# A mixture of a dense and a gathered expert layer: groups of two columns, three more gather tiles, earlier transposes, larger packets

## The chip, the cores and the metric

The kernel runs on one core of a Trainium2 chip. A core has TensorE (PE), VectorE (DVE), ScalarE (ACT), GpSimd (POOL) and SyncE (SP), which each work through their own instructions in a fixed order, and 16 DMA engines. The metric is the device time of one execution in microseconds (us); the median of several runs is compared.

## What is computed

A block of a network for 1024 tokens of 1024 channels: a mixer (sliding means and a gated part), and then a layer of 16,384 experts of which each token uses 128 (8 heads with 16 choices each). The second part, cut to what matters:

```python
def peer_ffn(h, wq, keys, u_tab, v_tab):        # block of 128 tokens
    q = (xb @ wq).reshape(T, PEER_HEADS, 2, D_HALF)
    s = jnp.einsum('thpd,phkd->thpk', q, keys)
    s_top, i_top = lax.top_k(s, PEER_TOPK)
    ...
    idx = jnp.take_along_axis(cand_i, best_pos, axis=-1)
    gate = jax.nn.softmax(best_s, axis=-1)
    u = u_tab[idx]
    v = v_tab[idx]
    act = jax.nn.gelu(jnp.einsum('td,thkd->thk', xb, u))
    return jnp.einsum('thk,thkd->td', gate * act, v)
```

All values are float32. The two tables u_tab and v_tab (peer_u, peer_v) hold 16,384 rows of 4 KB each.

## The kernel before

The tokens are eight blocks of 128. Blocks 2 to 5 (512 tokens) are done densely: every expert is computed for them, as 128 columns of 128 experts, and a gate that is zero for the experts not chosen is multiplied in. Blocks 0, 1, 6 and 7 are done sparsely: the chosen rows are gathered from the tables.

Ahead of both stands the mixer and the scoring. `project` (line 159) multiplies by the weights w_in, w_out and wq; each call loads two tiles w of 512 KB (line 164) in four buffers, with runs of 256 floats, 1 KB. It notes its last matmul in the list `marks`. Scoring gives per block the chosen experts (`pick`, line 383), and `turn` (line 465) transposes them.

The gate of the dense part is made by `gates_dense` (line 557): for four tokens at a time VectorE writes one-hot rows (oh), ScalarE scales them, TensorE multiplies them into a 128x128 map per token; 32 tokens make a tile gs of 2 MB that goes to G in DRAM (line 580). G is laid out by group of four columns first, so that a write goes out in runs of 512 B, and the load gc of four columns (line 647) reads 1 MB that lies together, in runs of 512 B.

`dense` (line 612) walks over the 128 columns. For each it loads raw_u and raw_v (512 KB each, three buffers together, lines 636 and 641), splits each into a high and a low part (ACT writes uh or vh, VectorE writes ul or vl, line 131), makes 24 matmuls into mu (`mm3`, lines 138 to 140: three products for each of 8 slices), then the gelu (ACT, line 652), the product with the gate (VectorE, line 653) and the split of that into wh and wl. When GROUP = 3 columns are ready, `down` (line 623) makes for each of 8 output parts 9 matmuls into one tile mm of the on-chip sums, and VectorE adds that into hD (line 631). vh, vl, wh and wl have GROUP buffers each.

A sparse block b has two halves. `sparse_u` (called Ub, line 494): 128 gathers of one row per token (a tile of 128 x 1024, 0.5 MB, issued by GpSimd, line 483), each followed by a product with a sum on VectorE (junk, line 504); then w is made and transposed into wT (lines 511 and 513). `sparse_v` (Vb, line 516): 32 quads; GpSimd copies a column of wT into one of four small tiles wz (line 523), gathers four tiles, and TensorE makes eight matmuls with them into po (line 534). The last closes the block (`finish`, line 548).

The gathered rows lie in ROWS = 7 tiles rowt and, once the first stage's memory is free, also in VROWS = 4 tiles rowv. Where U and V halves run together, U uses rowv and V uses rowt (line 680); else both are used in turn. EARLY and LATE (lines 56 and 57) say in which order the halves are written: U0, then V0 with half of U1 in the first stage; then, spread over the columns of `dense`, the rest of U1, V1 with U6, V6 with U7, and V7. The program is written in that order, and a scheduler (Tile, with its own model of times) puts the instructions of each engine into the final order; `anchors` (line 814) hold a transposition of w or a quad behind a chosen entry of `marks`.

Of the kernel before, what the change touches and what calls it, by code (L numbers as in the profile page):

```python
# [8 lines left out]
F32 = mybir.dt.float32  # L9
# [8 lines left out]
P = 128  # L18
# [3 lines left out]
HALF = 512  # L22
# [5 lines left out]
NK = 128  # L28
# [4 lines left out]
WC = 256  # L33
# [6 lines left out]
ND = N * len(MIDDLE)  # L40
DBLK = ND // P
d0 = D0 // P
GROUP = 3
TB = 4
GT = 32
GI = 4
# [5 lines left out]

ROWS, VROWS = 7, 4
QUAD = 4

EARLY = ({"U0": 128}, {"V0": 128, "U1": 64})
LATE = ({"U1": 64}, {"V1": 128, "U6": 128}, {"V6": 128, "U7": 128}, {"V7": 128})
# [6 lines left out]
def hybrid_block(ctx: ExitStack, tc: tile.TileContext, t: dict, out: bass.AP):  # L64
# [21 lines left out]
    wz = []  # L86
    for i in range(4):
        z = const.tile([P, 4, 63], F32, name=f"wz{i}")
        nc.gpsimd.memset(z, 0.0)
        wz.append(z)  # L90
# [17 lines left out]

    G = dram.tile([NK // GI, ND // GT, P, GI, GT], F32, name="G")

# [48 lines left out]
    def project(fr, name, col, xs, by_token):  # L159

        ws = []
        for half in range(2):
            w = fr.tile([P, 4, WC], F32, name="w", bufs=4)
            nc.sync.dma_start(w, t[name][half * HALF:(half + 1) * HALF, col:col + WC]
                              .rearrange("(c p) e -> p c e", p=P))
            ws.append(w)
        res = []
        for x in xs:
            dst = ps.tile([P, 2, N], F32, name="mm")
            for i in range(2):  # L170
                part = slice(i * P, (i + 1) * P)
                for c in range(NDC):
                    w = ws[c // 4][:, c % 4, :]
                    lhs, rhs = (x[:, c, part], w) if by_token else (w[:, part], x[:, c, :])
                    mm = nc.tensor.matmul(dst[:, i, :], lhs, rhs, start=c == 0, stop=c == NDC - 1)  # L175
            res.append(dst)
        marks.append(mm.ins)
        flush()
        return res
# [336 lines left out]
    def sparse_v(b):  # L516
# [4 lines left out]
        for j in range(32):  # L521
            z = wz[j % len(wz)]
            nc.gpsimd.tensor_copy(z[:, :, 31:32], wg[:, :, j:j + 1])

            rows_ = []
            for g in range(QUAD):
                rows_.append(gather("peer_v", idxT[:, g * 32 + j:g * 32 + j + 1], j))
                if g < QUAD - 1:
                    yield
            with behind(f"V{b}", j) or tc.high_priority():  # L530
                first = None
                for g, (r, _) in enumerate(rows_):
                    for q in range(2):
                        mm = nc.tensor.matmul(po[g * 32:(g + 1) * 32, q * HALF:(q + 1) * HALF],  # L534
                                              z[:, g, 31 - j:63 - j], r[:, q * HALF:(q + 1) * HALF],
                                              start=j == 0, stop=j == 31)
                        first = first or mm
# [19 lines left out]
    def gates_dense(gp, b):  # L557

        iT = turned[b]
        for part in range(P // GT):  # L560
            kb = (b - d0) * (P // GT) + part
            gs = gp.tile([P, NK, GT], F32, name="gs", bufs=2)
            for t0 in range(0, GT, TB):
# [9 lines left out]
                for i in range(TB):  # L573
# [5 lines left out]
                yield  # L579
            nc.sync.dma_start(G[:, kb].rearrange("a i b t -> i a (b t)"),  # L580
                              gs.rearrange("i (a b) t -> i a (b t)", b=GI))

# [29 lines left out]
    def dense(de, xdh, xdl):  # L612
# [3 lines left out]
        with tc.tile_pool(name="da", bufs=2, side="right", reuse_waits="tile") as da:  # L616
# [17 lines left out]
            for c in range(NK):  # L634
# [10 lines left out]
                if c % GI == 0:  # L645
                    gc = da.tile([P, ND // GT, GI, GT], F32, name="gc")
                    nc.sync.dma_start(gc.rearrange("i k b t -> i k (b t)"),
                                      G[c // GI].rearrange("k i b t -> i k (b t)"))
                p = ps1.tile([P, ND], F32, name="mu", bufs=2)
# [163 lines left out]
    rts.close()  # L813
    anchors.update({"U0": [marks[BEHIND[0]]], "V0": marks[BEHIND[0]::BEHIND[1]]})
    for _ in sparse(EARLY):
# [52 lines left out]
```

## Time and profile before

| what | us |
|---|---|
| median of three runs | 2639.56 |
| the three runs | 2629.94 to 2653.57 |
| the profiled execution | 2627.74 |
| its span, first to last instruction | 2625.9 |
| PE busy / DVE busy / POOL busy / ACT busy | 2415.2 / 1851.3 / 1264.0 / 766.9 |

The profile is of one execution. Busy time is the time in which an engine has at least one instruction at work; DMA share is the mean busy share of the 16 DMA engines, which can come out a little above 1 where packets overlap. Granted clock 1.00 is TensorE at 2.4 GHz, the lower level is 1.2 GHz. A wait is idle time of an engine, put down to what ended it.

### The profile page before, as it was taken

How to read it: one execution, taken by the hardware profiler on the slowest of the kernel's cores; microseconds unless marked ns; L12 is line 12 of the kernel's file. 1: busy time of each engine (PE TensorE's matmuls, PEld its weight loads, DVE VectorE, ACT ScalarE, POOL GpSimd, SP SyncE). 2: the span in 40 equal slices, each digit the busy share in tenths (PEclk: the TensorE clock that was granted, in tenths of full speed). 3: DMA queues.
4: the chain of work that ended last, by engine and by line, in shares of the span. 5: the costliest groups of instructions: out<-in, count | busy, mean ns of one | idle time of the engine just before them, and what ended most of it. 6: DMA issues, size and time to landing. Idle time of an engine off the chain costs nothing.

```text
span 2625.9 us, 34296 instructions
## 1 busy us (share of the span) xinstructions
PE 2415.2 (92%) x11968; PEld 1861.7 (71%) x11968; DVE 1851.3 (71%) x4251; ACT 766.9 (29%) x1420; POOL 1264.0 (48%) x1228
## 2 busy tenths in 40 slices
PE   7997999889985669999999999999999999999993
PEld 6886788767763547788777777777777777776660
DVE  2389979987978956799766766666677667664332
ACT  2221011247754632222222222222222222222110
POOL 0034744034455544455655565555555555644553
PEclk9998999999987789999999999999999999999997
DMA  7677999579998898999999999999989999988986
GB/s 242 219 245 231 376 340 305 181 247 364 328 327 287 286 344 291 333 343 352 344 354 356 350 332 349 350 351 337 365 327 348 361 333 349 349 333 321 324 317 240
DMA packets 348397, 835.65 MB, mean 318 GB/s; under 512 B 25153, under 2 KB 160833, under 8 KB 348225
## 3 DMA queue, kind: packets, MB, share of 16 engines
q0 software_dynamic: 147456, 536.94, 55.4%
q1 hardware_dynamic: 200768, 296.53, 33.0%
q8 instruction: 95, 1.56, 0.2%
q14 instruction: 78, 0.63, 0.1%
HBM read 787.23 MB, written 46.14 MB: 317 GB/s over the span
## 4 chain that ended last, share of the span: by engine, by line
PE 67%; DVE 15%; DMA 10%; issue 4%; ACT 1%; POOL 1%; SPq 0%; POOLq 0%; DVEq 0%; ACTq 0%
PE mm L138 8%; PE mu L140 8%; PE mm L139 8%; PE mu L138 8%; PE mm L140 8%; PE mu L139 8%; PE po L534 8%; PE mm L175 8%; DVE junk L504 3%; DVE oh L567 2%; DMA raw_u<-uT 2%; DMA rowt<-peer_u,idx 2%; DVE rest L375 1%; DMA rowv<-peer_u,idx 1%; DMA rowv<-peer_v,idxT 1%
## 5 line engine op out<-in xcount | busy, mean ns | idle before, releaser
L483 POOL DMA_INDIRECT rowt<-peer_v,idxT x448 | 511.0, 1141 | 649.1 <-PE po L534 393.6
L483 POOL DMA_INDIRECT rowt<-peer_u,idx x224 | 274.6, 1226 | 357.0 <-DVE top L373 165.4
L483 POOL DMA_INDIRECT rowv<-peer_u,idx x288 | 355.6, 1235 | 156.4 <-DVE junk L504 96.0
L138 PE MATMUL mm<-vh,wh 128*128 128x512 f32 x1024 | 398.1, 395 | 17.2 <-ACT wh L130 17.0
L138 PE MATMUL mu<-xdh,uh 128*128 128x512 f32 x1024 | 401.3, 392 | 4.0 <-ACT uh L130 4.0
L140 PE MATMUL mu<-xdh,ul 128*128 128x512 f32 x1024 | 401.7, 392 | 0.5 <-DVE ul L131 0.5
L139 PE MATMUL mm<-vl,wh 128*128 128x512 f32 x1024 | 400.5, 392 | 0.0
L139 PE MATMUL mu<-xdl,uh 128*128 128x512 f32 x1024 | 400.2, 391 | 0.0
L504 DVE SCALAR_TENSOR_TENSOR junk<-rowv,h 128x1024 bf16<-128x1024 f32 x288 | 351.5, 1221 | 60.2 <-DMA rowv<-peer_u,idx 57.8
L631 DVE TENSOR_TENSOR hD<-hD,mm 128x512 f32<-128x512 f32 x344 | 226.3, 683 | 213.6 <-PE mm L140 213.2
L140 PE MATMUL mm<-vh,wl 128*128 128x512 f32 x1024 | 374.1, 391 | 0.1
L504 DVE SCALAR_TENSOR_TENSOR junk<-rowt,h 128x1024 bf16<-128x1024 f32 x224 | 272.3, 1215 | 28.1 <-DMA rowt<-peer_u,idx 26.8
L652 ACT ACTIVATE a<-mu 128x512 f32<-128x512 f32 x128 | 76.3, 596 | 600.4 <-PE mu L140 600.0
L138 PEld LDWEIGHTS mm<-vh,wh 128*128 128x128 f32 x1024 | 193.3, 189 | 79.9 <-ACT wh L130 19.4
L534 PE MATMUL po<-rowt,wz 128*32 128x512 f32 x1792 | 232.4, 611 | 17.1 <-DMA rowt<-peer_v,idxT 13.6
L140 PEld LDWEIGHTS mu<-xdh,ul 128*128 128x128 f32 x1024 | 192.2, 188 | 59.2 <-issue 8.4
L138 PEld LDWEIGHTS mu<-xdh,uh 128*128 128x128 f32 x1024 | 192.2, 188 | 55.1 <-issue 10.9
L140 PEld LDWEIGHTS mm<-vh,wl 128*128 128x128 f32 x1024 | 191.9, 188 | 49.6 <-issue 8.4
L139 PEld LDWEIGHTS mu<-xdl,uh 128*128 128x128 f32 x1024 | 192.2, 188 | 48.0 <-issue 8.4
L139 PEld LDWEIGHTS mm<-vl,wh 128*128 128x128 f32 x1024 | 193.4, 189 | 44.5 <-issue 4.2
L131 DVE SCALAR_TENSOR_TENSOR ul<-raw_u,uh 128x1024 fp32r<-128x1024 f32 x128 | 156.4, 1222 | 44.4 <-ACT uh L130 42.7
L130 ACT ACTIVATE vh<-raw_v 128x1024 fp32r<-128x1024 f32 x128 | 130.0, 1048 | 176.4 <-PE mm L140 149.9
(162 smaller groups left out, 3323.0 us busy)
## 6 DMA issues: line engine op xcount, KB each, us to landing
raw_u<-uT SPq DMA_DIRECT2D x128, 512.0 KB, 7.0
raw_v<-peer_v SPq DMA_DIRECT2D x128, 512.0 KB, 6.9
G<-gs SPq DMA_DIRECT2D x16, 2048.0 KB, 16.8
w<-wq SPq DMA_DIRECT2D x48, 512.0 KB, 6.9
w<-w_in SPq DMA_DIRECT2D x36, 512.0 KB, 4.7
w<-w_out SPq DMA_DIRECT2D x24, 512.0 KB, 7.2
h<-x SPq DMA_DIRECT2D x16, 512.0 KB, 11.6
rowt<-peer_v,idxT POOLq DMA_INDIRECT x448
```

Of the source, the lines that this page charges most:

```text
L130: nc.scalar.activation(hi, src, AF.Copy)
L131: nc.vector.scalar_tensor_tensor(lo, src, 1.0, f32(hi), op0=ALU.mult, op1=ALU.subtract)
L138: nc.tensor.matmul(dst, lh, rh, start=first and c == 0, stop=False)
L139: nc.tensor.matmul(dst, lh, rl, start=False, stop=False)
L140: nc.tensor.matmul(dst, ll, rh, start=False, stop=last and c == n - 1)
L175: mm = nc.tensor.matmul(dst[:, i, :], lhs, rhs, start=c == 0, stop=c == NDC - 1)
L483: ins = nc.gpsimd.indirect_dma_start(out=rowt, out_offset=None, in_=t[table], in_offset=bass.IndirectOffsetOnAxis(ap=ids, axis=0))
L504: nc.vector.scalar_tensor_tensor(junk, r, 1.0, h, op0=ALU.mult, op1=ALU.mult, accum_out=act[:, j:j + 1])
L534: mm = nc.tensor.matmul(po[g * 32:(g + 1) * 32, q * HALF:(q + 1) * HALF], z[:, g, 31 - j:63 - j], r[:, q * HALF:(q + 1) * HALF], start=j = ...
L567: nc.vector.tensor_tensor(oh, iota_k[:, None, None, :].to_broadcast([P, 2, TB, NK]), iT[:, 0:2, tok:tok + TB, None].to_broadcast([P, 2, TB ...
L631: nc.vector.tensor_add(hq, hq, p)
L652: nc.scalar.activation(a, p, AF.Gelu_apprx_tanh)
```

## The change

Five things are changed. GROUP is 2 instead of 3: `down` runs every second column, with 6 matmuls for each of its 8 output parts, and there are two buffers of vh, vl, wh and wl. ROWS is 8 instead of 7, VROWS is 7 instead of 4, and there are three tiles wz instead of four. In EARLY 16 gathers of U1 stand between U0 and V0, and the transposition of block 0's w is held behind `marks[1]` instead of `marks[4]`. In `sparse_v` the copy into wz comes behind the four gathers of its quad. And the weights w are packed on the host so that each partition's part of a tile is one run of 4 KB, and G is laid out by 32 tokens, partition, column and token, so that gs is written in one run of 16 KB a partition, while gc still reads runs of 512 B.

```diff
-GROUP = 3
+GROUP = 2
...
-ROWS, VROWS = 7, 4
+ROWS, VROWS = 8, 7
 QUAD = 4
 
-EARLY = ({"U0": 128}, {"V0": 128, "U1": 64})
+EARLY = ({"U0": 128}, {"U1": 16}, {"V0": 128, "U1": 48})
...
-    for i in range(4):
+    for i in range(3):
         z = const.tile([P, 4, 63], F32, name=f"wz{i}")
...
-    G = dram.tile([NK // GI, ND // GT, P, GI, GT], F32, name="G")
+    G = dram.tile([ND // GT, P, NK, GT], F32, name="G")
...
-            nc.sync.dma_start(w, t[name][half * HALF:(half + 1) * HALF, col:col + WC]
-                              .rearrange("(c p) e -> p c e", p=P))
+            nc.sync.dma_start(w.rearrange("p c e -> p (c e)"), t[name][col // WC, half])
...
         for j in range(32):
-            z = wz[j % len(wz)]
-            nc.gpsimd.tensor_copy(z[:, :, 31:32], wg[:, :, j:j + 1])
 
             rows_ = []
             for g in range(QUAD):
                 rows_.append(gather("peer_v", idxT[:, g * 32 + j:g * 32 + j + 1], j))
                 if g < QUAD - 1:
                     yield
+            z = wz[j % len(wz)]
+            nc.gpsimd.tensor_copy(z[:, :, 31:32], wg[:, :, j:j + 1])
...
-            nc.sync.dma_start(G[:, kb].rearrange("a i b t -> i a (b t)"),
-                              gs.rearrange("i (a b) t -> i a (b t)", b=GI))
+            nc.sync.dma_start(G[kb].rearrange("i k t -> i (k t)"), gs.rearrange("i k t -> i (k t)"))
...
-                                      G[c // GI].rearrange("k i b t -> i k (b t)"))
+                                      G[:, :, c:c + GI, :].rearrange("k i b t -> i k (b t)"))
...
-    anchors.update({"U0": [marks[BEHIND[0]]], "V0": marks[BEHIND[0]::BEHIND[1]]})
+    anchors.update({"U0": [marks[1]], "V0": marks[BEHIND[0]::BEHIND[1]]})
...
+    def packed(w):
+
+        w = np.asarray(w)[0]
+        return c(w.reshape(2, 4, P, w.shape[1] // WC, WC).transpose(3, 0, 2, 1, 4).reshape(-1, 2, P, 4 * WC))
...
-        "w_in": c(np.asarray(w_in)[0]),
+        "w_in": packed(w_in),
```

w_out and wq are packed in the same way.

The scheduler makes a new order for every engine. At the end of TensorE's order of before stand these rows (mm is a part of `down`, a po row is one quad with a tile of rowv or rowt).

```order
L138 MATMUL mm<-vh,wh 128x512
L139 MATMUL mm<-vl,wh 128x512
L140 MATMUL mm<-vh,wl 128x512
L534 MATMUL po<-rowv,wz_87 32x512 x8
L534 MATMUL po<-rowt,wz_89 32x512 x8
L534 MATMUL po<-rowv,wz_91 32x512 x8
L534 MATMUL po<-rowt,wz_93 32x512 x8
L534 MATMUL po<-rowv,wz_87 32x512 x8
L534 MATMUL po<-rowt,wz_89 32x512 x8
L534 MATMUL po<-rowv,wz_91 32x512 x8
L534 MATMUL po<-rowt,wz_93 32x512 x8
```

And these stand there now, at the end of TensorE's order of the changed kernel.

```order
L139 MATMUL mm<-vl,wh 128x512
L140 MATMUL mm<-vh,wl 128x512
L138 MATMUL mm<-vh,wh 128x512
L139 MATMUL mm<-vl,wh 128x512
L140 MATMUL mm<-vh,wl 128x512
L138 MATMUL mm<-vh,wh 128x512
L139 MATMUL mm<-vl,wh 128x512
L140 MATMUL mm<-vh,wl 128x512
```

The eight quads that stood behind the last column are gone from there: the last quad now stands where 100.7 columns have had their matmuls into mu.

On VectorE, in the stretch of columns that V1 and U6 share, the order of before has this (hD_7475 to hD_7478 are the four blocks of the dense output, in two halves each; junk is a product with a gathered tile).

```order
L631 TENSOR_TENSOR hD_7475<-hD_7475,mm 128x512 x2
L631 TENSOR_TENSOR hD_7476<-hD_7476,mm 128x512 x2
L131 SCALAR_TENSOR_TENSOR ul<-raw_u,uh 128x1024
L653 TENSOR_TENSOR a<-a,gc 128x512
L631 TENSOR_TENSOR hD_7477<-hD_7477,mm 128x512 x2
L631 TENSOR_TENSOR hD_7478<-hD_7478,mm 128x512
L131 SCALAR_TENSOR_TENSOR wl<-a,wh 128x512
L131 SCALAR_TENSOR_TENSOR vl<-raw_v,vh 128x1024
L504 SCALAR_TENSOR_TENSOR junk,act<-rowv,h 128x1024
L131 SCALAR_TENSOR_TENSOR vl<-raw_v,vh 128x1024
L631 TENSOR_TENSOR hD_7478<-hD_7478,mm 128x512
L504 SCALAR_TENSOR_TENSOR junk,act<-rowv,h 128x1024 x3
```

VectorE's order of the changed kernel in the same stretch, where the four blocks are hD_7473 to hD_7476:

```order
L629 TENSOR_TENSOR hD_7473<-hD_7473,mm 128x512 x2
L503 SCALAR_TENSOR_TENSOR junk,act<-rowv,h 128x1024
L629 TENSOR_TENSOR hD_7474<-hD_7474,mm 128x512 x2
L503 SCALAR_TENSOR_TENSOR junk,act<-rowv,h 128x1024 x3
L629 TENSOR_TENSOR hD_7475<-hD_7475,mm 128x512
L503 SCALAR_TENSOR_TENSOR junk,act<-rowv,h 128x1024
L629 TENSOR_TENSOR hD_7475<-hD_7475,mm 128x512
L629 TENSOR_TENSOR hD_7476<-hD_7476,mm 128x512 x2
L131 SCALAR_TENSOR_TENSOR vl<-raw_v,vh 128x1024
L651 TENSOR_TENSOR a<-a,gc 128x512
L131 SCALAR_TENSOR_TENSOR wl<-a,wh 128x512
L131 SCALAR_TENSOR_TENSOR ul<-raw_u,uh 128x1024
```

The eight additions of a group now come every second column, and more products stand beside fewer columns: U6's 128 products are spread over some 25 columns, where they were spread over some 45.

On GpSimd, where U0 ends and V0 begins, the order of before has this (peer_u gathers are U0's and then U1's, peer_v gathers are V0's, the copies are the waits for wT).

```order
L483 DMA rowt<-peer_u,idx 128x1024 x129
L483 DMA rowt<-peer_v,idxT 128x1024 x4
L483 DMA rowt<-peer_u,idx 128x1024 x2
L483 DMA rowt<-peer_v,idxT 128x1024 x3
L523 COPY wz_87<-wT 128x4
L523 COPY wz_89<-wT 128x4
L523 COPY wz_91<-wT 128x4
L523 COPY wz_93<-wT 128x4
```

GpSimd's order of the changed kernel at the same place:

```order
L482 DMA rowt<-peer_u,idx 128x1024 x145
L482 DMA rowt<-peer_v,idxT 128x1024 x4
L482 DMA rowt<-peer_u,idx 128x1024
L482 DMA rowt<-peer_v,idxT 128x1024 x2
L528 COPY wz_87<-wT 128x4
L528 COPY wz_89<-wT 128x4
L528 COPY wz_91<-wT 128x4
L482 DMA rowt<-peer_v,idxT 128x1024 x2
```

Sixteen gathers of U1 moved in front of V0's first gathers.

## Rows read from the trace of the kernel before

**Rows 1.** The page's 40 slices: DMA share in tenths, and GB/s.

```profile
DMA  7677999579998898999999999999989999988986
GB/s 242 219 245 231 376 340 305 181 247 364 328 327 287 286 344 291 333 343 352 344 354 356 350 332 349 350 351 337 365 327 348 361 333 349 349 333 321 324 317 240
```

**Rows 2.** Busy time of each engine in stretches from 560 us on.

```profile
core 0: us, PE busy (x) PEld busy (x) DVE busy (x) ACT busy (x) POOL busy (x), PEclk, DMA share, GB/s
560.00:985.00 425.00, 328.61 (x1944) 252.28 (x1945) 337.37 (x876) 256.56 (x695) 210.80 (x177) 0.88 0.94 319
985.00:1237.00 252.00, 252.00 (x1153) 200.53 (x1152) 205.02 (x310) 70.28 (x90) 123.79 (x101) 1.00 0.91 328
1237.00:1793.00 556.00, 553.44 (x2650) 413.50 (x2649) 389.80 (x569) 142.43 (x183) 320.26 (x288) 1.00 0.94 349
1793.00:2349.00 556.00, 552.79 (x2642) 411.71 (x2641) 388.17 (x561) 141.58 (x181) 316.05 (x288) 1.00 0.94 346
2349.00:2562.00 213.00, 212.00 (x1110) 147.61 (x1114) 86.26 (x115) 43.93 (x55) 104.31 (x124) 0.99 0.87 318
2562.00:2626.00 64.00, 18.52 (x124) 5.09 (x116) 13.36 (x67) 5.74 (x10) 20.59 (x25) 0.72 0.64 235
```

**Rows 3.** TensorE's timeline: start, length, line, operation; 31 matmuls left out.

```profile
1606.36 0.39 PE L138 MATMUL mm<-vh,wh 128*128 128x512 f32 x1
...
1613.62 0.39 PE L140 MATMUL mm<-vh,wl 128*128 128x512 f32 x1
1613.93 1.94 PE L534 MATMUL po<-rowt,wz 128*32 128x512 f32 x16
1615.81 0.50 PE L138 MATMUL mm<-vh,wh 128*128 128x512 f32 x1
```

**Rows 4.** Lines 511, 513: durations in ns, first and last start; waits are EVENT_SEMAPHORE.

```profile
L511 PEldq EVENT_SEMAPHORE  x3: 51/51/51, 1237.3 to 2348.3; - x3
...
L513 DVE COPY wT<-wt x4: 268/280/285, 526.0 to 2349.4; 128x128 f32<-128x128 f32 x4
L513 DVEq EVENT_SEMAPHORE  x2: 21/21/21, 1793.3 to 2348.9; - x2
```

**Rows 5.** The same view as rows 2, for two stretches of 40 us.

```profile
1811.00:1851.00 40.00, 39.45 (x195) 28.85 (x185) 25.94 (x38) 10.85 (x14) 23.19 (x22) 1.00 1.03 396
2159.00:2199.00 40.00, 40.00 (x198) 29.09 (x197) 26.94 (x39) 10.61 (x14) 21.23 (x22) 1.00 1.03 398
```

**Rows 6.** DMA: two queues (packets, MB, share), then loads (KB each, us to landing).

```profile
q0 software_dynamic: 147456, 536.94, 55.4%
q1 hardware_dynamic: 200768, 296.53, 33.0%
...
raw_u<-uT SPq DMA_DIRECT2D x128, 512.0 KB, 7.0
...
w<-wq SPq DMA_DIRECT2D x48, 512.0 KB, 6.9
```

**Rows 7.** Groups: busy us, mean ns of one, idle before and what ended it.

```profile
L504 DVE SCALAR_TENSOR_TENSOR junk<-rowv,h 128x1024 bf16<-128x1024 f32 x288 | 351.5, 1221 | 60.2 <-DMA rowv<-peer_u,idx 57.8
L631 DVE TENSOR_TENSOR hD<-hD,mm 128x512 f32<-128x512 f32 x344 | 226.3, 683 | 213.6 <-PE mm L140 213.2
L504 DVE DVE_READ_ACCUMULATOR junk<-rowv,h 128x1 f32 x288 | 23.3, 81 | 0.0
```

**Rows 8.** Waits from 500 to 560 us: total us, times, longest.

```profile
POOL wz L523 <- DVE wT L513: 52.5, 1, 52.5
```

**Rows 9.** The chain that ended last, from 2540 us on: start, us, what.

```profile
2561.29 2.03 PE po L534 x16
...
2567.13 6.44 DMA rowv<-peer_v,idxT
...
2601.41 5.19 PE po L534 x32
2606.62 1.23 DVE h L545
...
2620.51 1.28 DVE hD L554
```

More of the change, by code (lines that the diff above doesn't have):

```diff
@@ L849 @@
         "sgu_b": c(np.asarray(sgu_b)[0]),
-        "w_out": c(np.asarray(w_out)[0]),
+        "w_out": packed(w_out),
         "norm2_g": c(np.asarray(norm2_g)[0]),
-        "wq": c(np.asarray(peer_wq)[0]),
+        "wq": packed(peer_wq),
         "keysT": c(np.asarray(peer_keys)[0].transpose(1, 0, 3, 2).reshape(NLIST, P, NK)),
```

## The prediction

> **What bounds the kernel now.** Four views were read, in this order. The page's slices show the DMA engines nearly full from about 300 us to 2550 us [rows 1]. The windows by stage show what TensorE and VectorE do meanwhile [rows 2]. I cut them at the times at which a sparse block's weights are transposed (lines 511 and 513), because that ends one block's U half and opens its V half: 526 us for block 0, 1237 for block 1, 1793 for block 6, 2349 for block 7 [rows 4]. From 985 us to 2562 us TensorE is busy for all but a few microseconds, at a granted clock of 1.00, which is the 2.4 GHz level [rows 2]. TensorE bounds the dense stage.
>
> The price of its work is read from the timeline [rows 3]. From 1606.36 to 1613.62 us 33 matmuls start, so one takes 7.26/32 = 0.227 us. A column has 48 (24 up, 24 down): 10.88 us. A quad of four gathered V tiles puts 2.19 us between the dense matmuls around it, less 0.23 for the matmul itself: 1.96 us. Check: counted in the order of the instructions, 44.4 columns and 32 quads stand between the transposes of blocks 1 and 6; 44.4 x 10.88 + 32 x 1.96 = 546 us, measured 556.
>
> The second fact is in the same row: DMA is at 0.94 of its engines' time, moving 349 GB/s. A gather brings 128 rows of 4 KB, 0.524 MB; a column needs raw_u and raw_v (0.524 MB each) and a quarter of gc (1.05 MB per four columns), 1.311 MB. 256 gathers and 44.4 columns are 134.2 + 58.2 = 192 MB, and 556 us x 349 GB/s is 194. So TensorE and DMA are balanced within a few per cent, and whoever asks for more gathers per column makes DMA the bound. VectorE has room (390 of 556 us), GpSimd too (320; the same instructions now get 458).
>
> After the last dense matmul TensorE waits: quads run at 2561, each wait is a gather that could start only when its tile came free (6.4 us to land), the last quads run at 2601, and 20 us of closing work follow [rows 9].
>
> **The change, part by part.**
>
> *The order.* This decides. More tiles for gathered rows let the program's scheduler place gathers, and the quads that use them, beside fewer columns, and each engine keeps its written order. Counted in it, the transposes for blocks 1, 6 and 7 stood after 25.6, 70.0 and 114.1 columns and now stand after 24.7, 52.0 and 82.0; the last quad stood behind column 128 and now stands at column 100.7. So V1 with U6 (256 gathers) has 27.3 columns where it had 44.4, V6 with U7 has 30.0 where it had 44.1, V7 has 18.7, and 27.3 columns at the end have no gather at all. TensorE's work is the same. The bytes of a stretch are now:
> - V1 and U6: 134.2 + 27.3 x 1.311 = 170 MB. TensorE needs 27.3 x 10.88 + 63 = 360 us.
> - V6 and U7: 134.2 + 39.3 = 173.5 MB. TensorE needs 326 + 63 = 389 us.
> - V7: 67.1 + 24.5 = 91.6 MB. TensorE needs 203 + 63 = 266 us.
>
> The rate of a full DMA is bounded by 349 GB/s (the whole stretch at share 0.94 [rows 2]) and 398 GB/s (40 us at share 1.03 [rows 5]). I take 349/0.94 = 371, because a queue that never empties is what the share of 1 means, while the 398 stands beside idle stretches before and after it. Then V1/U6 takes 458 us (427 to 487), V6/U7 468 us (436 to 497); both are over TensorE's time. V7 at 371 needs 247 us, under TensorE's 266; I take 271, since both are near full. The last 27.3 columns take 297 us of TensorE alone, with DMA two thirds idle. What is lost is that the transfers of the last stretch cannot help the crowded ones: the tiles hold only 15 gathers (7.9 MB, 21 us).
>
> The Trainium skill ("DMA: Bandwidth & Descriptors", Specifications) gives about 358 GB/s as what HBM grants a core. By it the two stretches would take 475 and 485 us, 34 more. The trace has 396 and 398 over 40 us [rows 5], so the measurement decides.
>
> TensorE's clock falls where it idles: 0.88 granted in the mean (some of the time at the lower level, 1.2 GHz) over the stage in which it was busy 329 of 425 us [rows 2]. At 0.88 the 360 us become 409, still under 458, so I charge nothing.
>
> *Sums over two columns.* 512 additions into hD instead of 344: 168 x 0.683 = 115 us of VectorE [rows 7]. In the two crowded stretches it has room: of the 390 us [rows 2], 128 products of 1.30 are 166, so a column takes 5.0; now 166 + 27.3 x (5.0 + 0.9) is 327 of 458. Before column 24.7 it has less: 30 extra additions, 21 us, beside 205 busy of 252 [rows 2]; I take 7 (0 to 21). Only two columns' vh, vl, wh, wl exist, so ACT and VectorE must refill them between the last matmul of one group and the first of the next; in the last 27 columns, some 13 groups, I take 10 us (0 to 30). Elsewhere DMA hides it.
>
> *Block 0's transposes, and 16 products between.* GpSimd stands 52.5 us before wz until wT is there [rows 8]; the transpose now comes some 48 matmuls earlier, 16 of U1's gathers stand before the wait, and the copies come behind the gathers. By the order, 26 quads instead of 24 and 176 products instead of 167 precede the dense work: 17 gathers, 8.9 MB, 24 us of DMA, moved forward into a stage at share 0.94. *Large packets.* w comes in 4 KB runs instead of 1 KB, G is written in 16 KB runs instead of 512 B. The queue with the small pieces moved 296.53 MB in 33.0% of the span, 342 GB/s, the gathers 536.94 MB in 55.4%, 369 [rows 6]; 90 MB (56.6 of w, 33.5 of G) at 369 instead of 342 frees 19 us of DMA. A w lands in 6.9 us, a raw_u of 4 KB runs in 7.0 [rows 6], so no wait for w is shortened. Freed and added DMA time cancel; dense work starts 10 us earlier (40 earlier if GpSimd's wait comes off, 20 later if the 16 products at 1.30 us delay VectorE, which has 16 x 1.30 = 21 us more to do there [rows 7]).
>
> *Sum.* Dense start 985 - 10 = 975; to column 24.7, 252 x 24.7/25.6 + 7 = 250; 458; 468; 271; 297; groups 10; closing 20: 2749 us of span against 2625.9. The execution lasts 1.8 us longer than its span, and the median of the runs shown is 11.8 above that execution (2639.56 against 2627.74): 2763 us.
>
> **Rivals.**
> - *TensorE stays the bound* and the deeper tiles do what they promise: 975 + 250 + 360 + 389 + 266 + 297 + 20 = 2557, 2571 as a median. For it: TensorE is the bound now, and the wait after the last matmul goes. Against it: 170 MB in 360 us is 472 GB/s, and no stretch shows over 398. Chance 0.05.
> - *DMA nearly keeps up*: to equal the old time the two stretches may take 803 us together, 428 GB/s. For it: share 1.03 can be exceeded if more is queued. Against: as above. About 2640. Chance 0.05.
> - *gc becomes slow.* The pieces of one partition of gc now lie 2 MB apart instead of 64 KB. If that doubles its DMA time, the 14 loads in the crowded stretches (15 MB, at 342 GB/s 44 us) cost 44 more: 2807. Against it: gc moves 512 B pieces either way, and G's scattered writes ran in a stage that moved 319 GB/s at share 0.94 [rows 2]. Chance 0.2. The Trainium skill ("DMA: Bandwidth & Descriptors", Latency and other measured facts) states that a row pitch of 2 MiB in HBM brought copies down to 164 GB/s; no row here shows such a pitch.
> - *VectorE becomes the bound*: its 115 us fall on the path of a kernel that DMA does not hold: 2571 + 115 = 2686. It decides from the point where products and additions together fill VectorE, as they come near to before 1237, with 205 of 252 us [rows 2]. Chance 0.05.
>
> **How the numbers follow.** DMA as the bound of the two stretches has 0.65, with 2763; the rate alone moves that from 2700 to 2821, and the smaller terms by -50 to +65 together. They will not all fall one way, so the range is 2680 to 2850; it holds the third and the fourth rival too, and leaves out the first two and the far ends. Faster or slower means by over 1%, about what a measurement of this kernel can tell: faster 0.05 (the first rival), same 0.05 (the second), slower 0.9 (the rest).
>
> **What would show it.** Right: transposes for blocks 1, 6, 7 near 1225, 1683 and 2151 us; TensorE under 85% busy between them, DMA share at 0.98 or more, TensorE waiting for rowt, raw_u or raw_v; no gather after some 2420 us, and DMA near 120 GB/s from there. Wrong: TensorE full between 1237 and the second transpose, or a rate over 420 GB/s there; VectorE full; or gc landing in twice its time, which would be the third rival.

## The result, and the profile after

The changed kernel takes 2778.25 us (median of 4 runs, 2768.14 to 2790.86) where the kernel before took 2636.26 us in the same job (4 runs, 2629.94 to 2653.57). The ratio is 1.0527, with a 95% interval of 1.0489 to 1.0565: slower by 142 us. The forecast was 2763, with a range of 2680 to 2850. The profiled execution took 2768.14 us, with a span of 2766.2.

The slices of the changed kernel's page, DMA share and GB/s, answer to [rows 1].

```profile
DMA  6577998687988878879999999999999899953432
GB/s 251 204 263 252 399 345 310 229 300 287 332 302 334 322 278 304 289 281 356 388 376 373 363 381 369 382 374 378 394 344 396 302 351 337 342 175 108 130 107 76
```

The transposes have moved (lines 510 and 512 are 511 and 513 of before, [rows 4]): block 1's is at 1250.4, block 6's at 1705.9, block 7's at 2177.

```profile
L510 PEldq EVENT_SEMAPHORE  x3: 51/51/51, 1250.4 to 2177.0; - x3
...
L512 DVE COPY wT<-wt x4: 269/284/291, 497.7 to 2177.5; 128x128 f32<-128x128 f32 x4
L512 DVEq EVENT_SEMAPHORE  x2: 21/21/21, 1705.9 to 2177.5; - x2
```

The windows of the changed kernel, cut at these times, at the last quad and at the last dense matmul, have the columns of [rows 2].

```profile
560.00:985.00 425.00, 326.99 (x1947) 242.24 (x1948) 329.68 (x864) 252.84 (x691) 219.21 (x181) 0.88 0.86 317
985.00:1250.00 265.00, 251.02 (x1088) 196.51 (x1087) 212.21 (x325) 67.07 (x87) 105.47 (x87) 0.97 0.81 280
1250.00:1706.00 456.00, 401.44 (x1912) 279.08 (x1910) 330.54 (x499) 93.69 (x120) 320.10 (x287) 0.97 1.00 375
1706.00:2177.00 471.00, 413.89 (x1916) 284.64 (x1914) 333.49 (x504) 93.58 (x121) 319.94 (x289) 0.96 0.98 373
2177.00:2445.00 268.00, 265.38 (x1400) 183.53 (x1400) 119.59 (x158) 60.30 (x76) 123.59 (x146) 0.99 0.90 327
2445.00:2752.00 307.00, 306.90 (x1353) 253.80 (x1354) 181.16 (x251) 90.72 (x117) 0.00 (x0) 1.00 0.33 107
2752.00:2767.00 15.00, 1.43 (x7) 0.85 (x5) 9.73 (x45) 1.83 (x4) 0.00 (x0) 0.65 0.35 140
```

Two things are to be seen. From 1250 to 2177 the DMA engines are full (share 1.00 and 0.98, 375 and 373 GB/s), while TensorE, which was busy for all but 3 us of 556 in [rows 2], now works for 401 of 456 us and 414 of 471; VectorE and GpSimd have more than 120 us of room in each. And from 2445 to 2752 TensorE is full, GpSimd does nothing, and DMA moves 107 GB/s: the last 27 columns run with no gather beside them.

The waits between 1250 and 2177 us (total us, times, longest) show how the full DMA reaches TensorE.

```profile
PEld mm L138 <- ACT wh L130: 80.3, 36, 9.3
...
PE mm L138 <- ACT wh L130: 58.6, 31, 8.9
...
PE mm L139 <- DVE vl L131: 12.2, 5, 4.7
PE mu L140 <- DVE ul L131: 12.2, 9, 3.2
```

TensorE has run out of columns that are ready. vl and ul are split straight from the loads; wh, the longest wait, is split from the product with the gate and comes behind the 24 up matmuls of its column. Which load had held that column up the waits do not name. None of them is put down to gc, but 39.6 us of VectorE's waits before the product with the gate have no cause in the profile (34.7 in the same stretches of old_g, below).

The chain that ended last is dense work from the last quad on, where that of before had gathers between its last quads [rows 9].

```profile
2441.38 3.61 PE po L533 x32
...
2742.15 0.91 PE mm L138 x4
2746.68 0.24 PE mm L140
2746.95 0.70 DVE hD L629
2747.69 0.50 PE mm L138
2748.65 0.23 PE mm L138
2753.20 0.24 PE mm L140
2753.47 0.69 DVE hD L629
2754.74 1.19 DVE hD L553
```

The DMA queues, for [rows 6]:

```profile
q0 software_dynamic: 147456, 536.94, 51.9%
q1 hardware_dynamic: 144960, 296.53, 30.3%
```

And the group of the additions, for [rows 7]:

```profile
L629 DVE TENSOR_TENSOR hD<-hD,mm 128x512 f32<-128x512 f32 x512 | 334.3, 683 | 273.1 <-PE mm L140 240.5 <-issue 11.9 <-remote 9.7
```

The same bytes go in 144,960 packets instead of 200,768, and 168 more additions cost 334.3 - 226.3 = 108 us of VectorE; yet the kernel is slower.

### The profile page after: what moved, and what is told of

Its sections match the earlier page's. It is cut to its first block, busy times and chain, and to the rows that moved or that the text cites. A ratio compares the mean times of both kernels' runs of the same rounds, so it can differ in the third digit from the quotient of the medians.

```text
span 2766.2 us, 34479 instructions
## 1 busy us (share of the span) xinstructions
PE 2465.5 (89%) x11968; PEld 1871.3 (68%) x11968; DVE 1958.6 (71%) x4419; ACT 765.7 (28%) x1418; POOL 1274.9 (46%) x1227
## 3 DMA queue, kind: packets, MB, share of 16 engines
q1 hardware_dynamic: 144960, 296.53, 30.3%
## 4 chain that ended last, share of the span: by engine, by line
PE 54%; DVE 21%; DMA 12%; issue 8%; ACT 2%; POOL 1%; another core or an unknown queue 0%; SPq 0%; DVEq 0%; POOLq 0%; ACTq 0%
PE mm L138 7%; PE mm L139 7%; PE mm L174 7%; PE mu L140 6%; PE mu L138 6%; PE mm L140 6%; PE mu L139 6%; PE po L533 6%; DVE junk L503 5%; DMA raw_u<-uT 3%; DMA rowv<-peer_u,idx 3%; DVE oh L566 2%; DMA rowt<-peer_u,idx 2%; DMA rowt<-peer_v,idxT 2%; DVE hD L629 1%
## 5 line engine op out<-in xcount | busy, mean ns | idle before, releaser
L482 POOL DMA_INDIRECT rowt<-peer_v,idxT x448 | 537.8, 1200 | 421.6 <-PE po L533 203.8
L629 DVE TENSOR_TENSOR hD<-hD,mm 128x512 f32<-128x512 f32 x512 | 334.3, 683 | 273.1 <-PE mm L140 240.5
L482 POOL DMA_INDIRECT rowv<-peer_u,idx x288 | 349.0, 1212 | 174.0 <-DVE junk L503 103.9
L139 PE MATMUL mm<-vl,wh 128*128 128x512 f32 x1024 | 411.8, 405 | 13.8 <-DVE vl L131 13.6
L533 PE MATMUL po<-rowt,wz 128*32 128x512 f32 x1792 | 242.6, 625 | 25.6 <-DMA rowt<-peer_v,idxT 19.5
L651 DVE TENSOR_TENSOR a<-a,gc 128x512 f32<-128x512 f32 x128 | 88.3, 691 | 217.4 <-ACT a L650 122.8
L139 PEld LDWEIGHTS mm<-vl,wh 128*128 128x128 f32 x1024 | 200.1, 195 | 60.0 <-DVE vl L131 18.3
L140 PEld LDWEIGHTS mm<-vh,wl 128*128 128x128 f32 x1024 | 197.5, 193 | 52.2 <-issue 5.0
```

Source lines behind the costliest of these rows:

```text
L139: nc.tensor.matmul(dst, lh, rl, start=False, stop=False)
L140: nc.tensor.matmul(dst, ll, rh, start=False, stop=last and c == n - 1)
L482: ins = nc.gpsimd.indirect_dma_start(out=rowt, out_offset=None, in_=t[table], in_offset=bass.IndirectOffsetOnAxis(ap=ids, axis=0))
L629: nc.vector.tensor_add(hq, hq, p)
L651: nc.vector.tensor_mul(a.rearrange("i (k t) -> i k t", t=GT), a.rearrange("i (k t) -> i k t", t=GT), gc[:, :, c % GI, :])
```

## The experiments

The theory is crowding: with room for four more tiles (ROWS and VROWS together go from 11 to 15, where the title has three more) the order puts the gathers of V1, U6, V6 and U7 beside fewer columns, DMA becomes the bound there, and the columns left over run alone at the end. The rivals are that the cost is in the added work (additions, two columns' buffers), or in the new layout of G, which gc reads in pieces 2 MB apart. All medians are of 4 to 11 runs of the kernel; the ratios are to the kernel before in the same job (2633 to 2641 us).

| run | median us | ratio to before | 95% interval |
|---|---|---|---|
| the change | 2778.25 | 1.0527 | 1.0489 to 1.0565 |
| tiles_back | 2635.73 | 0.9995 | 0.9978 to 1.0012 |
| paced | 2745.87 | 1.0418 | 1.0378 to 1.0458 |
| balanced | 2690.49 | 1.0206 | 1.0160 to 1.0253 |
| balanced_whole | 2647.30 | 1.0046 | 1.0025 to 1.0067 |
| old_g | 2723.32 | 1.0319 | 1.0278 to 1.0360 |
| balanced_old_g | 2634.96 | 1.0002 | 0.9981 to 1.0023 |
| tiles_back_old_g | 2624.75 | 0.9956 | 0.9935 to 0.9977 |
| front_only | 2613.42 | 0.9907 | 0.9872 to 0.9942 |
| front_old_g | 2595.88 | 0.9829 | 0.9806 to 0.9853 |
| packets | 2633.73 | 0.9969 | 0.9954 to 0.9985 |
| early | 2603.17 | 0.9864 | 0.9843 to 0.9885 |
| early32 | 2597.05 | 0.9863 | 0.9842 to 0.9885 |

**The tiles alone** (tiles_back). All of the change stays but the four tiles.

```diff
-ROWS, VROWS = 8, 7
+ROWS, VROWS = 7, 4
```

> The changed kernel with ROWS = 7 and VROWS = 4 as before; groups of two columns, the packets, the earlier transposes and the 16 products stay. Counted in its order, the transposes for blocks 1, 6 and 7 stand after 26.0, 68.0 and 114.0 columns, as before the change. Crowding (too many gathers beside too few columns make DMA the bound): the 140 us go, 2635 to 2665 us. Additions (168 more additions on VectorE and the refill of two columns' buffers): they stay, 2740 to 2780 us. Layout of G (gc slow): stays too, since gc reads the new layout, 2720 or more.

Measured 2635.73: the whole loss of 142 us goes with the four tiles. The windows of tiles_back show what comes back.

```profile
1253.00:1810.00 557.00, 552.45 (x2649) 410.23 (x2648) 423.31 (x630) 141.44 (x178) 306.72 (x293) 1.00 0.96 350
1810.00:2363.00 553.00, 550.16 (x2627) 411.89 (x2626) 423.05 (x628) 142.89 (x182) 306.12 (x284) 1.00 0.97 350
```

TensorE is full again, with 350 GB/s beside it. The additions, the groups of two and the new layout of G are still in this kernel, so they do not make the 142 us by themselves. What groups of two cost beside the deeper tiles was not run; without those it is 22 us (front_only, below).

**The same tiles with the gathers spread** (paced, balanced, balanced_whole). If crowding is the cause, the tiles must be harmless where the gathers stand beside as many columns as before. In paced a quad is held behind the last `up` matmul of the column in whose loop it is written, and a product behind that column's gate product, so that the scheduler cannot pull them ahead.

```diff
+    pace = {}
+    def held(engine):
+        return tc.issue_after(pace[engine]) if pace.get(engine) else None
...
-            nc.vector.scalar_tensor_tensor(junk, r, 1.0, h, op0=ALU.mult, op1=ALU.mult, accum_out=act[:, j:j + 1])
+            with held("DVE") or ExitStack():
+                nc.vector.scalar_tensor_tensor(junk, r, 1.0, h, op0=ALU.mult, op1=ALU.mult, accum_out=act[:, j:j + 1])
...
-            with behind(f"V{b}", j) or tc.high_priority():
+            with behind(f"V{b}", j) or held("PE") or tc.high_priority():
...
-                mm3(p, [(uh[:, i, :], ul[:, i, :]) for i in range(NDC)], xd)
+                pace["PE"] = mm3(p, [(uh[:, i, :], ul[:, i, :]) for i in range(NDC)], xd)
...
-                nc.vector.tensor_mul(a.rearrange("i (k t) -> i k t", t=GT), a.rearrange("i (k t) -> i k t", t=GT), gc[:, :, c % GI, :])
+                pace["DVE"] = nc.vector.tensor_mul(a.rearrange("i (k t) -> i k t", t=GT), a.rearrange("i (k t) -> i k t", t=GT), gc[:, :, c % GI, :]).ins
```

> The changed kernel with all its tiles, but each quad is ordered behind the last up matmul of the column it is written beside, and each product behind that column's product with the gate: an order, no new wait. The transposes then stand after 24.7, 58.7 and 104.8 columns, the last quad at 126. Crowding: 34 columns with 256 gathers are 179 MB, 480 us by DMA; 46 columns 564 us by TensorE; 21 columns 294; 2 more 22; closing 15; from 1250 us on that is 2625 us of span, 2638 in the median. Additions or layout of G: nothing they name is changed, 2778 as the changed kernel.

Measured 2745.87: only 32 us come back, and the 2638 that crowding had forecast were missed by 108, so this run by itself speaks for neither theory. By the order its transposes stand after 24.7, 58.7 and 104.8 columns: the hold keeps a quad behind the column that the program wrote it in, and the loop itself had written V1 and U6 within 34 columns. That was in the forecast (480 us for these 34, 564 for the next 46); measured between the transposes were 520 and 605, and V7 was some 30 over as well. The next two runs show where a good part of this went: the main group of quad matmuls is busy for 303.2 us in paced and for 242.6 in the changed kernel. balanced also sets the columns by which each phase has been written.

```diff
-    steps = sum(sum(phase.values()) for phase in LATE)
+    ends = (24, 67, 110, 127)
+    due, start = [], 0
+    for phase, end in zip(LATE, ends):
+        n = sum(phase.values())
+        due += [start + (i + 1) * (end - start) / n for i in range(n)]
+        start = end
...
-        while done * (NK - GROUP) < min(c + 1, NK - GROUP) * steps:
+        while done < len(due) and due[done] <= c + 1:
```

> As paced, and the gathers of the last stage are written so that each stretch has its share of columns: transposes after 25.0, 68.0 and 110.8 columns, the last quad at 128. Crowding: every stretch is under the rate of a full DMA (190 MB in 531 us are 359 GB/s), so TensorE sets it: 1250 + 531 + 529 + 250 + closing 20 is 2580 us of span, about 2593 in the median, up to 2620 if the last quads wait. Additions or layout of G: 2778 as the changed kernel, less at most 20 us.

Measured 2690.49: 88 us back, and 98 short of what was expected. The page's group of quads shows part of the rest; this is balanced:

```profile
L540 PE MATMUL po<-rowt,wz 128*32 128x512 f32 x1792 | 294.1, 619 | 14.9 <-DMA rowt<-peer_v,idxT 14.9
```

In the kernel before the same 1792 matmuls are busy for 232.4 us. The held quads had lost their high priority, and the scheduler cut them up with dense matmuls between (179 rows of quad matmuls in TensorE's order instead of 139). balanced_whole gives the held quads of the late blocks their priority back.

```diff
-            with behind(f"V{b}", j) or held("PE") or tc.high_priority():
+            with behind(f"V{b}", j) or held("PE") or ExitStack(), ExitStack() if f"V{b}" in anchors else tc.high_priority():
```

> As balanced, but each quad keeps the priority that it has in the changed kernel, so that fewer are cut by dense matmuls (139 rows of quads in TensorE's order instead of 179; 139 in the changed kernel). The columns of the transposes are the same, 25.0, 68.0, 110.9. Crowding, with the excess of balanced put down to cut quads: some 36 us in each of the two long stretches and 20 later go, 2590 to 2620 us. If the deeper tiles cost something of their own even where DMA is not full: 2690 as balanced.

Measured 2647.30, 43 us less; the quads' group is down by 294.1 - 245.0 = 49 us:

```profile
L540 PE MATMUL po<-rowt,wz 128*32 128x512 f32 x1792 | 245.0, 630 | 13.1 <-issue 6.4 <-DMA rowt<-peer_v,idxT 4.8 <-POOL wz L535 1.9
```

With eight and seven tiles, 131 of the 142 us are back, by the order alone: the tiles cost little by themselves (11.6 us over tiles_back), and what they cost goes with the columns beside the gathers. The windows of balanced_whole between the transposes show the rates and what is still missing.

```profile
1248.00:1804.00 556.00, 547.11 (x2594) 404.00 (x2593) 414.62 (x613) 137.41 (x174) 308.81 (x285) 0.99 0.93 340
1804.00:2378.00 574.00, 553.37 (x2606) 406.51 (x2605) 420.12 (x629) 139.17 (x178) 317.84 (x291) 0.99 0.93 342
```

TensorE lacks 9 and 21 us of being full, and the time expected (2590 to 2620) was missed by 27. Part of that is the new layout's (next); the rest stays open.

**The layout of G** (old_g, then three pairs). The change with G as before:

```diff
-    G = dram.tile([ND // GT, P, NK, GT], F32, name="G")
+    G = dram.tile([NK // GI, ND // GT, P, GI, GT], F32, name="G")
...
-            nc.sync.dma_start(G[kb].rearrange("i k t -> i (k t)"), gs.rearrange("i k t -> i (k t)"))
+            nc.sync.dma_start(G[:, kb].rearrange("a i b t -> i a (b t)"),
+                              gs.rearrange("i (a b) t -> i a (b t)", b=GI))
...
-                                      G[:, :, c:c + GI, :].rearrange("k i b t -> i k (b t)"))
+                                      G[c // GI].rearrange("k i b t -> i k (b t)"))
```

> The changed kernel with G laid out as before (by group of four columns first; gs written in runs of 512 B, gc read from 1 MB that lies together). The order is the changed kernel's within a column (24.7, 53.0, 82.0; last quad 99.9). Crowding: 2770 to 2790 us, as the changed kernel. Layout of G: the time falls by 20 to 50 us, to 2730 to 2758, and the stretches between the transposes get shorter than 456 and 471 us.

Measured 2723.32: the new layout costs 55 us in the changed kernel (2778.25 - 2723.32), more than either theory had. The windows of old_g, cut at its own transposes (1229.8, 1690, 2138):

```profile
985.00:1230.00 245.00, 235.56 (x1028) 186.55 (x1029) 204.62 (x314) 65.72 (x86) 99.84 (x84) 0.99 0.86 301
1230.00:1690.00 460.00, 415.21 (x1935) 288.09 (x1937) 336.08 (x512) 94.20 (x120) 322.22 (x290) 0.96 1.00 379
1690.00:2138.00 448.00, 405.45 (x1882) 279.44 (x1875) 327.13 (x498) 91.00 (x118) 317.91 (x287) 0.96 1.00 385
2138.00:2395.00 257.00, 256.77 (x1374) 177.57 (x1372) 114.90 (x147) 58.92 (x74) 121.11 (x145) 1.00 0.90 334
```

The crowded stretches are still there, at share 1.00, so crowding holds without the new layout. But it is then smaller: with the old layout the deeper tiles cost 99 us (2723.32 - 2624.75, tiles_back_old_g below) and with the new one 142, so some 44 of the 142 come only where both meet. Between the two profiled executions (spans 2766.2 and 2725.0) lie 41 us: 20 by block 1's transposition, 19 in the two crowded stretches together (927 us against 908), 11 in V7, and some 8 back at the end. Is it the crowding that makes the layout dear? (The two orders differ by a column at most.) Three kernels without crowding were run with the old layout too: tiles_back, balanced_whole (with the phases' ends at 24, 66, 108 and 125 columns) and, below, front_only. Their edit is that of old_g.

> tiles_back with G laid out as before. If the new layout of G costs at the start of the dense stage and in its loads whatever the order: 2605 to 2625 us. If it costs only where DMA is full and gathers crowd: 2636 as tiles_back.

> As balanced_whole with G laid out as before, and the last quads two columns earlier (66.1, 109.0, last 126.5). Crowding with gc as a second price: old_g gained 55 us where DMA was full for 900 us; here DMA is not full, so 10 to 30 us under balanced_whole, 2570 to 2600. If gc's layout costs only where DMA is full: the same as balanced_whole.

Measured 2624.75 and 2634.96: the layout costs 11 us and 12 us there (the 12 are not the layout's alone, as the last quads of balanced_old_g also stand two columns earlier). If the layout costs something in any order, 2605 to 2625 and 2570 to 2600 were expected. The first is at that range's end; the second missed its range, but the difference to balanced_whole lies in the 10 to 30 that were forecast for it. The kernel before took 2633 to 2641 us in the different jobs, so differences between runs of different jobs are uncertain by some microseconds.

In the pair of tiles_back the first activation of a dense column comes at 943.7 us with the new layout and at 928.6 with the old one: all of the cost lies before the dense columns, while G is written. In each of the four pairs TensorE, VectorE, ScalarE and GpSimd run the same instructions in the same order up to 945 us, so this part is no matter of the order. It shows in VectorE's wait for gathered rows between 560 and 930 us, with the new layout and the old one of the pair of tiles_back:

```profile
DVE junk L503 <- DMA rowt<-peer_u,idx: 35.4, 13, 6.3
...
DVE junk L503 <- DMA rowt<-peer_u,idx: 23.2, 12, 5.6
```

The other pairs have 23.9 against 15.5 (the change and old_g), 37.4 against 23.3 (front_only and front_old_g) and 19.4 against 11.0 us (balanced_whole and balanced_old_g). Why these waits are longer beside G's new writes was not tested.

The packets of the traces also show that gc's reads have changed: with the old layout gc comes in 16,384 packets of 2 KB, with the new one in 65,536 of 512 B. These are all packets between the transposes of blocks 1 and 7, in the changed kernel (927 us) and in old_g (908 us).

```profile
DMA packets 121767, 346.88 MB, mean 374 GB/s; under 512 B 10322, under 2 KB 41042, under 8 KB 121715
...
DMA packets 98723, 346.89 MB, mean 382 GB/s; under 512 B 10314, under 2 KB 10314, under 8 KB 98671
```

The bytes are the same. Of the 19 us, gc's packets make 8 (they take 56.2 against 48.6 us, spread over 16 engines), and some 10 are time in which DMA was not full (all packets take 917 of 927 us against 908 of 908).

**What the front part gives** (front_only, front_old_g, packets, early, early32). front_only is the change with seven and four tiles and groups of three.

```diff
-GROUP = 2
+GROUP = 3
...
-ROWS, VROWS = 8, 7
+ROWS, VROWS = 7, 4
```

> The changed kernel with ROWS = 7, VROWS = 4 and groups of three columns: only the packets, the earlier transposes, the 16 products and the three tiles wz are left of the change. Transposes after 24.0, 67.2 and 112.5 columns. Crowding: as before, 2636, plus or minus 15. Additions: 10 to 25 us under tiles_back, since 168 additions of 0.683 us go and VectorE is near full before the transpose of block 1.

Measured 2613.42: faster than before by 22 us (2635.88 in the same job), and 22 under tiles_back, which is what groups of two cost without crowding. With the old layout as well (front_old_g, the edit of old_g):

> The change with seven tiles for raw columns, four for the up factor and groups of three as before, and with block 0's gathered results laid out as before; what is left of the change is the packed first-layer loads, block 0's transposes written 16 columns in, and the 16 activations between them. If the new layout costs some 11 us wherever the transfers are not crowded, as in the two other pairs, about 2602 us, 11 under the same kernel with the new layout (2613). If that cost comes only with groups of two: 2613 us.

Measured 2595.88, ratio 0.9829 (0.9806 to 0.9853): faster than both kernels, by 1.7% than before and by 182 us than the change. Here the layout's price is 17.5 us (11 were expected). To see which part gives this, the packed weights and the early transposition (with its 16 gathers of U1) were each put into the kernel before, alone.

```diff
-            nc.sync.dma_start(w, t[name][half * HALF:(half + 1) * HALF, col:col + WC]
-                              .rearrange("(c p) e -> p c e", p=P))
+            nc.sync.dma_start(w.rearrange("p c e -> p (c e)"), t[name][col // WC, half])
```

> The kernel before with the first layer's weights loaded in large packets, and nothing else of the change. If no wait for these loads is shortened, as forecast: 2636 us, give or take 5. If the gain of the front part is that of the packets: 2615 to 2625 us.

```diff
-EARLY = ({"U0": 128}, {"V0": 128, "U1": 64})
+EARLY = ({"U0": 128}, {"U1": 16}, {"V0": 128, "U1": 48})
...
-    anchors.update({"U0": [marks[BEHIND[0]]], "V0": marks[BEHIND[0]::BEHIND[1]]})
+    anchors.update({"U0": [marks[1]], "V0": marks[BEHIND[0]::BEHIND[1]]})
```

> The kernel before with block 0's transposes written 16 columns in instead of later, and with the 16 activations that the change puts between; small packets, the old layout, seven and four tiles and groups of three as before. If the front's gain (22 us, and 11 more that the new layout takes back) comes from this move: 2600 to 2615 us. If it comes from the packets: 2636 us.

The packets give 7 to 8 us (2633.73 against 2640.7, ratio 0.9969), below 1% and nearly as forecast; the early transposition with its gathers gives 37 (2603.17, ratio 0.9864). Together they are the 45 us of front_old_g (2640.7 - 2595.88), which leaves nothing to see for the three tiles wz and the later copies. The chain of early shows where, and it is not where the forecast had looked.

```profile
2558.50 2.07 PE po L534 x16
...
2564.38 6.25 DMA rowv<-peer_v,idxT
2570.77 5.09 PE po L534 x32
2575.89 1.23 DVE h L545
```

The last dense matmul starts at 2558.0 instead of 2560.9: 3 us. But behind it the chain has one gather (2564 us), where that of before had three in turn (from 2567 us on [rows 9], 14 us apart), and the last quads end 31 us earlier (2575.9 against 2606.6): four quads stand behind the last column in its order, eight in that of before. The gathers that came forward are missing at the end. Does it go on? early32 is front_old_g with 32 gathers of U1 between instead of 16.

```diff
-EARLY = ({"U0": 128}, {"U1": 16}, {"V0": 128, "U1": 48})
+EARLY = ({"U0": 128}, {"U1": 32}, {"V0": 128, "U1": 32})
```

> The best version so far (seven and four tiles, groups of three, packed first-layer loads, the old layout of the gated results, 2595.9 us), with 32 of U1's gathers between U0 and V0 where it has 16. By the order the last quad then has two columns' work for the down matrix behind it, where four quads stood behind the last column. If the early move gains by the quads that no longer stand behind the last column, the 18 us between the last dense matmul and the end of the last quad go, and some of it comes back as the same gathers before the dense columns: 2580 to 2588 us, with the closing work straight behind the dense matmuls. If the gain of the early move came from GpSimd's filled wait alone, it is spent with 16: 2596 us; if the gathers only crowd the stage before the dense columns, more than 2600.

Measured 2597.05: no gain, where 2580 to 2588 were expected. Its chain ends in dense matmuls with no gather behind them, as the theory of the last quads had it:

```profile
2580.84 0.24 PE mm L140
2581.11 0.69 DVE hD L630
2582.38 1.20 DVE hD L553
```

But the last dense matmul comes 25 us later than in front_old_g (2580.7 against 2556.2), since the dense columns start later: the first column's ul is made at 869.2 us instead of 846.7. All of the gain at the end is paid at the start: 32 gathers win no more than 16. Other numbers were not run.

## Why the prediction was right

*Crowding* was the step that decided, and it held. Forecast were 458 and 468 us for the stretches V1/U6 and V6/U7; measured 456 and 471, moving 375 x 456 = 171 MB and 373 x 471 = 176 MB (forecast 170 and 173.5). V7 took 268 us (271). The columns without gathers took 307 us where 297 of TensorE and 10 for the refill of two columns' buffers were charged. That sum is right by luck: TensorE is busy for 306.9 of the 307 us and waits for no refill. It runs 1353 matmuls there, 655 of up and 698 of `down`, since `down` was nearly two columns behind when the last quad ran; the forecast had 27.3 columns of both, 1310. The granted clock was 0.97 and 0.96 in the crowded stretches, and nothing came of it, as TensorE had 55 us to spare in each. Two signs came out less sharply than forecast: TensorE was busy 88% of both stretches (forecast under 85%), and its longest waits were for wh, vl and ul, not for rowt. That the cause is the order that the tiles bring is shown from two sides: the tiles taken away (tiles_back), and the same tiles with the gathers spread (balanced_whole).

*The full DMA's rate* was taken as 371 GB/s. Measured are 375 and 373 with the new G and 379 and 385 with the old one, at share 1.00 or 0.98. The Trainium skill ("DMA: Bandwidth & Descriptors", Specifications) has some 358 GB/s as a core's limit; this case goes over it for 450 us at a time, and the measurement decides, as the prediction said.

*The start of the dense work* was missed: forecast 10 us earlier, measured 6 later (the first activation of a column at 949.0 us against 943.1). The block-1 transposition came at 1250.4 instead of 1225. The step that failed is "freed and added DMA time cancel" together with G's cheaper writes: with the old layout the transposition comes at 1229.8, so 20 of the 25 us are the layout's. The freed time is real, and by the packets more than the 19 us forecast: G's writes take 35 us less of the 16 engines' time (86 against 121 in old_g), the larger packets of w some 15 (packets against before). But it buys nothing: from 560 to 985 us DMA moves 317 GB/s at share 0.86 where it moved 319 at 0.94 [rows 2]. So DMA's time did not set the dense start. VectorE, busy for 330 of these 425 us, waited longer for its gathered rows between 560 and 930 us than in before (23.9 against 13.0 us).

*The third rival* had chance 0.2 and was priced at 44 us on top of the forecast, by gc's reads in the crowded stretches. The layout does cost 55 us (41 between the profiled executions), but only 19 of them in those stretches, so its size was near by luck and its place mostly was not. gc's DMA time did not double: over the whole kernel its packets take 121 us of 16 engines where they took 107 in old_g. The argument against this rival was wrong too: gc does not move 512 B pieces either way, since with the old layout its packets have 2 KB. Without the layout the sum would have been over the truth: old_g's span of 2725 us lies 24 under the 2749 of the forecast, 20 of them in V6/U7 (448 against 468) and 14 in V7 (257 against 271), with 10 back elsewhere. So the forecast stood near the result partly because a rate taken too low made up for a cost left out. The Trainium skill ("DMA: Bandwidth & Descriptors", Latency and other measured facts) has 164 GB/s for copies with a row pitch of 2 MiB between partitions. Here 2 MB lie between the pieces of one partition, and the partitions 16 KB apart, so the runs do not test that figure: gc is only 16 of the 347 MB of the two crowded stretches, and these differ by 4 and 12 GB/s between the layouts. Before the first read of gc at 954 us the layout can act only by G's writes, and behind it only by the reads, as every write must have ended; the runs show a loss on both sides (15 us before it in the pair of tiles_back, and in the changed kernel 6 before it, 949.0 against 943.3 for the first activation, and 35 behind). In the reads the smaller packets account for 8 of the 19 us in the crowded stretches; what makes the rest, and what lengthens the waits for gathers beside the writes, stays open.

*Two columns' groups* were charged 17 us (7 and 10). In the changed kernel the refill charged with 10 in the last stretch cost nothing, as said above, and the 7 were not measured apart. Without crowding they cost 22 (front_only against tiles_back), and of the 23 us by which the last quad ends later (2617.5 against 2594.4) only 7 are dense work (2582.9 against 2576.1); the rest is quads behind the last column, six in the one order and four in the other.

*The early transposition* was charged as 10 us of dense start. With its 16 gathers it is worth 37 in the kernel before, 28 of the 31 between the profiled spans (2625.9 and 2594.9) at the end; in the changed kernel, whose last quad stands 27 columns before the end, there is no such wait left to save. GpSimd's wait for wT did go, as the order said: 59.4 us in all over three waits before, 9.5 in one in early.

Of the other rivals, a bound of TensorE (2571) and a DMA that nearly keeps up (2640) fall by the measured 373 to 385 GB/s, and VectorE as the bound by its 331 of 456 us.

## What to carry to other kernels

More buffers are not only slack: where a scheduler fills them, they change which work stands beside which, and a balanced stage (here TensorE full and DMA at 0.94) can fall apart into one bound by DMA and one that leaves DMA idle, at the sum of both. So read the order by columns before and after, and divide the bytes of each stretch by a rate that the trace shows. And look for the gain of a moved wait at the far end too: work taken forward is missing from the tail, until what it delays at the start weighs as much.

## What was not expected

Cutting a quad up with dense matmuls costs TensorE time: the same 1792 matmuls are busy for 294.1 us in balanced and for 245.0 in balanced_whole, and the kernels lie 43 us apart. In the traces two dense matmuls start 0.23 us apart, but a quad's matmul starts 0.32 us behind a dense one, and a dense one 0.52 us behind a quad's, so every further cut pays for a change in each direction. And a layout that writes G in 16 KB runs instead of 512 B, with fewer packets and less DMA time in its queue (30.3% of 2766 us against 31.6% of 2725, 23 us), is slower in every one of four pairs: by 55, 17.5, 12 and 11 us. Larger packets on the write side had made the packets on the read side smaller, and the gathers that ran beside the writes were waited for longer.
